# Hybrid encoder layer on one core: the second row tile's LayerNorm moved ahead, v's partial products regrouped, PSUM places swapped

## The chip, the cores and the metric

One core of one Trainium2 chip runs the whole kernel. The metric is the time of one execution in device microseconds, as the median of several runs. An execution's own time is a little more than the span of its instructions, since it includes what lies around them.

## The reference

The input `x` has 1024 positions (a 16 x 64 grid) of 1024 channels, in float32. One LayerNorm (`emb_ln_g`, `emb_ln_b`) gives `h`. One layer follows: `proj = h @ w_in`, split by columns into q, k, v, z_attn, u, z_lru (512 each) and two merge gates (1024 each). Neighbourhood attention with a bias table works on q, k and v; a bidirectional gated linear recurrence works on u. Both results are gated, projected, merged with sigmoid gates and sent through `w_out`, and a second LayerNorm ends the layer:

```python
h = layer_norm(x, emb_ln_g, emb_ln_b)
proj = h @ w_in
q, k, v, z_a, u, z_b, g_a, g_b = jnp.split(proj, offs, axis=-1)
...
return layer_norm(ALPHA * x + out, ln_g, ln_b)
```

The change concerns the first of these steps alone: `h`, its transposed copy, and the first tiles of v and q.

## The kernel before, in words

**Tiles and stages.** The 1024 positions are eight row tiles of 128, numbered 0 to 7. Tile `i` is loaded (`load_x`), normalised on VectorE, stored for later (`keep`, to `h_d`), and turned by TensorE (`turn`) so that channels lie on partitions; a tile has two halves `kk` = 0, 1 of four 128-channel chunks each. Later stages, after about 62 us: the rest of v, q and k-like products, 16 pairs of wide projections in a seven-product scheme (`product`, from 105 us on), the recurrence beside them, then attention, the merges and the output projection.

**High and low parts.** Full precision is made from rounded operands: each float32 operand is split into a rounded high part (ScalarE copies) and a low part, the rest (VectorE or GpSimd subtracts). A product is high x high + low x high + high x low. For v of tile `i`, `v_part(i, kind, ks)` (line 322) issues one 128x512 matmul for each chunk in `ks`: kind `h` is high of h by high of the weight, `a` is low of h by high of the weight, `w` is high of h by low of the weight. Each v tile takes 24 such matmuls into one PSUM bank. They need `turn_hi` (line 278, ScalarE) or `turn_lo` (line 281, VectorE) of the tile's half, and `wv_hi` (line 194, ScalarE) or `wv_lo` (line 197, GpSimd) of the weight chunk. The eight weight chunks come in four transfers of two chunks.

**The first LayerNorm.** Scale and bias are spread into four PSUM banks `gps` (two halves of each). Tiles 0, 1 and 3 read them there: `ln_v(i, c)` (line 240) does one half on VectorE, with the statistics from `ln_stats` (line 216) and the square root from `ln_root` (line 226, ScalarE); `ln_sums` is both. The other tiles are scaled on ScalarE (`ln_scale`, line 248) and finished on GpSimd (`ln_g`, line 255), which reads copies of scale and bias in SBUF; `gb_copy(z, c)` (line 213, ScalarE) makes these, `z` = 0 for the scale and 1 for the bias. Where ScalarE and VectorE read the same PSUM bank, the later reader in program order waits for the earlier one.

**q.** `qk_load(m)` loads a 512 KB weight block into a single buffer, `qk_prep(m)` (line 177) splits it: `qk_hi` casts on ScalarE (line 171) and `qk_lo` subtracts on GpSimd. `qk_load(1)` can start when `qk_lo(0)` has read the buffer, and `qk_prep(1)` comes in ScalarE's order ahead of the high parts of tiles 2 and 3. `q_part(m, n)` multiplies half `n` of the positions; `q_hi` (ScalarE, line 355) and `q_lo` (VectorE, line 360) empty the bank, and the store goes out on SP.

**What sets the order.** Each engine works through its own list in the order in which the code calls the helpers (the order is written out by hand, from line 395 on), and so does the queue SP for the transfers. `warm_up(n)` (line 200) issues `n` matmuls on zeros, which keep TensorE busy while it waits. SP's list is: x0, the weight chunks, x1, more chunks, x2, q's block 0, x3, x4, the small parameters, store of h 0, x5, store of h 1, q's block 1, x6, stores of h 2 and h 3, and so on. x has five buffers, so x5 needs the buffer of x0, and its load waits until the store of h 0 has landed.

**PSUM places.** There are eight banks. While this first part runs, banks 0 to 3 are given out by a list written by hand (`places`, line 86): each call of `bank` takes the next number. Banks 4 to 7 hold `gps` and, after `psg.release()`, the turned tiles 2 to 7. The bank tiles are asked for in this order: clock, tp0_0, and then v0, tp0_1 and so on, as the code first uses them; from v4 on the order is v4, v5, v6, v7, q0_1, q1_1, q2_0, q2_1, q3_0, q3_1 (`q3_1` is `q_part(3, 1)`, the last of them). Then these pools are released, `psd` takes banks 0 and 1 and a pool of six (`ps6`, line 617) takes banks 2 to 7. Its first tile is the first product's accumulator `a11`, in bank 2. A tile in a reused bank waits for the readers of the tile that was there last.

Of the kernel before, what the change touches and what calls it, by code (L numbers as in the profile page):

```python
# [31 lines left out]
WARM = 18, 4, 6  # L32
# [35 lines left out]
def encoder_kernel(ctx, tc, x, gb1, gb, w_qk, w_v, w_s, w_ba, w_bb, w_gate, smalls, bias, w_out, out):  # L68
# [14 lines left out]
    hb12 = pool("hb12", "right")  # L83

    turns = []
    places = itertools.chain((0, 1, 2, 3, 0, 1, 2, 0, 2, 3, 1), itertools.cycle((2, 3, 0, 1)))

    def bank(name):
        if turns:
            return banks[0].tile([P, HALF], F32, tag=next(turns[0]), bufs=2, name=name)  # L90
        if banks[0] is ps0:
            return ps0.tile([P, HALF], F32, tag=f"b{next(places)}", bufs=1, name=name)
        return banks[0].tile([P, HALF], F32, tag="bank", name=name)
# [33 lines left out]
    def lo_of(eng, lo, full, hi):  # L127
        eng.tensor_tensor(lo, full, hi.bitcast(F32), ALU.subtract)  # L128
# [40 lines left out]
    def qk_hi(m):  # L169
        qk_w[m] = pair(wpl, [P, NK, P], f"wqk{m}", tag="w", bufs=2)  # L170
        A.copy(qk_w[m][0][:], qk_s[m][:])

    def qk_lo(m):
        hi, lo = qk_w[m]
        lo_of(G, lo[:], qk_s.pop(m)[:], hi[:])

    def qk_prep(m):
        qk_hi(m)
        qk_lo(m)
# [3 lines left out]
    def load_x(i):  # L183
        xs[i] = ln.tile([P, D], F32, tag="x", bufs=5, name=f"x{i}")
        if i == 0:
            for sl in halves:
                SP.dma_start(xs[i][:, sl], x[i][:, sl])
        else:
            SP.dma_start(xs[i][:], x[i])
# [4 lines left out]
    def wv_hi(k):  # L194
        A.copy(wv[0][k][:], wvs[k // 4][:, k % 4, :])

    def wv_lo(k):
        lo_of(G, wv[1][k][:], wvs[k // 4][:, k % 4, :], wv[0][k][:])

    def warm_up(n):  # L200
        for _ in range(n):
            PE.matmul(clock[:, :P], zero[:], zero[:], start=True, stop=True)
# [10 lines left out]
    def gb_copy(z, c):  # L213
        A.copy(gb_t[z][c][:], gps[z][c][:])

    def ln_stats(i):
        st, mv, e = (ln.tile([P, n], F32, tag=f"ln{n}{c}", bufs=2, name=f"ln{i}{c}")
                     for n, c in ((12, "t"), (2, "m"), (4, "e")))
        sts[i] = st, mv, e[:, 3:4], e[:, 0:3]
        sd, ve = sts[i][2:]  # L220
        for c in range(2):
            V.bn_stats(st[:, 6 * c:6 * c + 6], xs[i][:, halves[c]])
        V.bn_aggr(mv[:], st[:].rearrange("p (c s) -> p c s", c=2))
        V.tensor_scalar(ve[:, 0:1], mv[:, 1:2], EPS, -0.5, ALU.add, ALU.mult)

    def ln_root(i):
        st, mv, sd, ve = sts[i]
        A.activation(sd, mv[:, 1:2], AF.Sqrt, bias=eps_t[:])

    def ln_sums(i):  # L230
        ln_stats(i)
        ln_root(i)

    def ln_rstd(i):
        st, mv, sd, ve = sts[i]
        V.reciprocal(sd, sd)
        V.tensor_scalar(ve[:, 1:2], sd, sd, ve[:, 0:1], ALU.mult, ALU.mult)
        V.tensor_scalar(sd, ve[:, 1:2], 1.5, sd, ALU.add, ALU.mult)

    def ln_v(i, c):  # L240

        z, (st, mv, sd, ve), sl = xs[i], sts[i], halves[c]
        V.scalar_tensor_tensor(z[:, sl], z[:, sl], mv[:, 0:1], gps[0][c][:], ALU.subtract, ALU.mult)
        if c == 0:
            ln_rstd(i)
        V.scalar_tensor_tensor(z[:, sl], z[:, sl], sd, gps[1][c][:], ALU.mult, ALU.add)

    def ln_scale(i):

        z, (st, mv, sd, ve) = xs[i], sts[i]  # L250
        ln_rstd(i)
        V.tensor_scalar(ve[:, 2:3], mv[:, 0:1], -1.0, sd, ALU.mult, ALU.mult)
        A.activation(z[:], z[:], AF.Identity, bias=ve[:, 2:3], scale=sd)

    def ln_g(i):
        z = xs[i]
        for c in range(2):
            for w, op in enumerate((ALU.mult, ALU.add)):
                G.tensor_tensor(z[:, halves[c]], z[:, halves[c]], gb_t[w][c][:], op)

    def keep(i):
        SP.dma_start(h_d[i], xs[i][:])
# [3 lines left out]
    def turn(i, kk):  # L266
        tp = tps[i, kk] = bank(f"tp{i}_{kk}")
        for k4 in range(4):
            k = 4 * kk + k4
            PE.transpose(tp[:, k4 * P:(k4 + 1) * P], xs[i][:, k * P:(k + 1) * P], ident[:])  # L270

    def ti(i):
        return slice((i % 4) * P, (i % 4 + 1) * P)

    def tp4(i, kk):
        return tps[i, kk][:].rearrange("p (k t) -> p k t", k=4)

    def turn_hi(i, kk):
        A.copy(blocks[kk][i // 4][0][:, :, ti(i)], tp4(i, kk))  # L279

    def turn_lo(i, kk):
        hi, lo = blocks[kk][i // 4]
        lo_of(V, lo[:, :, ti(i)], tp4(i, kk), hi[:, :, ti(i)])
# [38 lines left out]
    def v_part(i, kind, ks):  # L322

        if i not in vos:
            vos[i], vn[i] = bank(f"v{i}"), 0
        for k in ks:
            a = blocks[k // 4][i // 4][kind == "a"][:, k % 4, ti(i)]
            PE.matmul(vos[i][:], a, wv[kind == "w"][k][:], start=vn[i] == 0, stop=vn[i] == 23)  # L328
            vn[i] += 1
# [3 lines left out]
    def v_hi(i):  # L333
        vs = outs["v", i] = ln.tile([P, H, 2, DH], F32R, tag="vs", bufs=2, name=f"vs{i}")
        A.copy(vs[:, :, 0, :], vos[i][:].rearrange("p (h d) -> p h d", d=DH))
# [11 lines left out]
    def q_part(m, n, cols=slice(0, HALF)):  # L347
        if (m, n) not in qos:
            qos[m, n] = bank(f"q{m}_{n}")
        run(mm3(qos[m, n][:, cols], [([t[:, 4 * kk + k, :] for t in qk_w[m]], [t[:, k, cols] for t in blocks[kk][n]])  # L350
                                     for kk in range(2) for k in range(4)]))
# [41 lines left out]
    K0, K1, KS, BOTH = range(4), range(4, 8), range(8), range(2)  # L393
# [28 lines left out]
    ln_v(0, 1)  # L422
    keep(0)
    load_x(5)
    turn(0, 1)
    warm_up(WARM[2])
    wv_hi(2)
    wv_hi(3)
    turn_hi(0, 1)
    turn_lo(0, 0)  # L430
    gb_copy(0, 0)
    wv_hi(4)
    wv_hi(5)
    ln_sums(1)
    turn_lo(0, 1)
    wv_hi(6)
    wv_hi(7)
    gb_copy(1, 0)
    for k in KS:
        wv_lo(k)  # L440
    qk_prep(0)
    for k in K0:
        v_part(0, "h", (k,))
        v_part(0, "a", (k,))
    v_part(0, "w", (0, 1))
    v_part(0, "h", (4, 5))
    v_part(0, "w", (2, 3))
    v_part(0, "h", (6, 7))
    v_part(0, "a", K1)
    ln_v(1, 0)  # L450
    ln_v(1, 1)
    keep(1)
    qk_load(1)
    load_x(6)
    turn(1, 0)
    turn_hi(1, 0)
    v_part(0, "w", (4, 5))
    v_part(1, "h", K0)
    turn(1, 1)
    for z in BOTH:  # L460
        gb_copy(z, 1)
    turn_hi(1, 1)
    v_part(0, "w", (6, 7))
    ln_stats(2)
    turn_lo(1, 0)
    ln_root(2)
    v_hi(0)
    ln_scale(2)
    turn_lo(1, 1)
    ln_g(2)  # L470
    v_part(1, "w", K0)
    v_part(1, "h", K1)
    v_part(1, "a", KS)
    v_part(1, "w", K1)
    ln_sums(3)
    q_part(0, 0, slice(0, 256))
    ln_v(3, 0)
# [525 lines left out]
    for slot in range(7 * N_PAIR + 4):  # L1003
        p, k = divmod(slot, 7)
# [183 lines left out]
    for unit in range(-NT, H * NT + PV_LAG):  # L1188
        h, c = divmod(unit, NT)
# [162 lines left out]
    for i in range(NT):  # L1352
        last = i == NT - 1
        load_z(i + 3)
        z = zs.pop(i)
# [115 lines left out]
```

## Time and profile before

| what | value |
|---|---|
| median of 3 runs | 678.17 us (678.04 to 678.44) |
| the profiled execution | 678.46 us |
| its span, first to last instruction | 676.7 us |
| TensorE matmul busy | 665.2 us (98%) |
| TensorE weight loads busy | 555.7 us (82%) |
| VectorE, ScalarE, GpSimd busy | 492.7, 364.5, 355.8 us |
| moved by DMA | 113.39 MB, mean 168 GB/s |
| mean granted TensorE clock | 0.997 |

PE is TensorE's matmuls, PEld its weight loads, DVE is VectorE, ACT ScalarE, POOL GpSimd, and SPq the queue that issues most transfers. In a row of the timeline the columns are the start in us, the duration, the engine, the line, the operation with output and input, and how many instructions are merged; in brackets stands the idle time before it and what ended it. A row of the stages (`A:B`) gives the length, and then the busy time of PE, PEld, DVE, ACT and POOL. In the chain of work that ended last, each row has a start, a duration and what was worked on.

### The profile page before, as it was taken

What the parts mean: (1) busy time and instruction counts of PE and PEld (TensorE: products, weight loads), DVE (VectorE), ACT (ScalarE), POOL (GpSimd) and SP (SyncE); (2) the same over time, 40 slices, a digit from 0 to 9 for tenths busy, and PEclk for the clock granted to TensorE, in tenths of its full rate; (3) what the DMA queues carried; (4) which work ended last, traced back from release to release, by engine and by line L of the source; (5) the groups of instructions that cost most, each with busy time, mean ns of one, the idle gap of its engine ahead of it and who ended that gap; (6) DMA issues with size and microseconds to landing.
All of it is one profiled execution on the core that took longest, in us unless ns stands there. A gap on an engine that the chain in (4) does not pass through costs nothing.

```text
span 676.7 us, 9344 instructions
## 1 busy us (share of the span) xinstructions
PE 665.2 (98%) x3201; PEld 555.7 (82%) x3201; DVE 492.7 (73%) x821; ACT 364.5 (54%) x612; POOL 355.8 (53%) x258
## 2 busy tenths in 40 slices
PE   8999999999999999999999999999999999999995
PEld 6888888888888887888788888888888878888884
DVE  6978747886998699879967785477787787443434
ACT  6554433256786676669576634477777554210110
POOL 6798632434677576567647444116155456334442
PEclk9999999999999999999999999999999999999998
DMA  8654353233434133431553456998793467412211
GB/s 326 244 179 170 122 206 126 77 110 123 125 128 144 40 103 115 170 126 48 195 178 122 173 191 254 316 366 296 255 323 132 162 220 281 178 62 94 93 63 62
DMA packets 48702, 113.39 MB, mean 168 GB/s; under 512 B 5056, under 2 KB 9744, under 8 KB 47120
## 3 DMA queue, kind: packets, MB, share of 16 engines
q1 hardware_dynamic: 48624, 112.81, 47.2%
q8 instruction: 25, 0.41, 0.3%
q14 instruction: 21, 0.17, 0.1%
q10 hardware_dynamic: 32, 0.01, 0.0%
HBM read 77.11 MB, written 35.68 MB: 167 GB/s over the span
## 4 chain that ended last, share of the span: by engine, by line
PE 89%; DVE 6%; DMA 2%; issue 1%; SPq 1%; ACT 0%; POOL 0%; DVEq 0%; POOLq 0%
PE a L134 30%; PE o L134 13%; PE mb L134 12%; PE s L134 11%; PE q L134 6%; PE v L328 6%; PE acc L1107 3%; PE s L1061 3%; PE pt L1083 3%; PE g L759 2%; DMA wqk_s<-in_w_qk_dram 2%; DVE ws_l L128 1%; PE tp L270 1%; DMA rsb<-rs_d 1%; DVE uc L717 1%
## 5 line engine op out<-in xcount | busy, mean ns | idle before, releaser
L134 PE MATMUL o<-wo_h,ml 128*128 128x512 f32 (+1 forms) x136 | 51.2, 377 | 0.0
L134 PE MATMUL o<-wo_l,mh 128*128 128x512 f32 (+1 forms) x136 | 51.2, 376 | 0.0
L134 PE MATMUL o<-wo_h,mh 128*128 128x512 f32 (+1 forms) x136 | 51.2, 376 | 0.0
L134 PE MATMUL a<-ht_h,ws_h 128*128 128x512 f32 x128 | 50.0, 390 | 0.0
L134 PE MATMUL a<-ht_l,ws_h 128*128 128x512 f32 x128 | 49.8, 389 | 0.0
L134 PE MATMUL a<-ht_h,ws_l 128*128 128x512 f32 x128 | 49.8, 389 | 0.0
L134 PE MATMUL a<-b_h,wa_h 128*128 128x512 f32 x128 | 49.8, 389 | 0.0
L134 PE MATMUL a<-b_h,wa_l 128*128 128x512 f32 x128 | 49.8, 389 | 0.0
L134 PE MATMUL a<-b_l,wa_h 128*128 128x512 f32 x128 | 49.8, 389 | 0.0
L1071 DVE CUSTOM_DVE_ANT_0 sc<-s,bias 128x384 f32<-128x384 f32 (+1 forms) x64 | 33.4, 522 | 21.6 <-PE s L1061 14.2
L1361 DVE SCALAR_TENSOR_TENSOR z<-z,o 128x512 f32<-128x512 f32 (+1 forms) x17 | 11.2, 656 | 51.0 <-PE o L134 51.0
L1091 ACT CAST pt_h<-pt 128x384 fp32r<-128x384 f32 x64 | 29.0, 453 | 25.3 <-PE pt L1083 17.3
L1371 POOL TENSOR_TENSOR z<-z,gb 128x1024 f32<-128x1024 f32 x7 | 16.8, 2400 | 48.5 <-ACT z L1370 48.5
L1076 ACT ACTIVATE p<-sc,summ 128x384 f32<-128x384 f32 (+1 forms) x64 | 37.8, 591 | 5.5 <-DVE summ L1071 5.3
L1340 ACT ACTIVATE sd<-mv,eps_z 128x1 f32<-128x1 f32 x8 | 2.4, 294 | 67.1 <-DVE mv L1366 67.1
L128 DVE TENSOR_TENSOR pt_l<-pt,pt_h 128x384 fp32r<-128x384 f32 x64 | 33.2, 519 | 2.1 <-ACT pt_h L1091 1.6
L328 PE MATMUL v<-wv,b_h 128*128 128x512 f32 x128 | 32.9, 398 | 0.6 <-ACT b_h L279 0.5
L867 POOL CAST wb_h<-wb 128x512 fp32r<-128x512 f32 x9 | 7.0, 779 | 47.4 <-DMA wb<-in_w_bb_dram 47.4
L1061 PE MATMUL s<-ks,qs 128*128 128x384 f32 (+1 forms) x128 | 31.4, 327 | 0.0
L1083 PEld LDWEIGHTS pt<-ident,p 128*128 128x128 f32 x176 | 23.1, 140 | 8.5
L1083 PE MATMUL pt<-ident,p 128*128 128x128 f32 x176 | 29.6, 272 | 0.0
L128 POOL TENSOR_TENSOR wb_l<-wb,wb_h 128x512 fp32r<-128x512 f32 x16 | 22.0, 1375 | 14.3 <-ACT wb_h L865 13.6
(438 smaller groups left out, 2204.2 us busy)
## 6 DMA issues: line engine op xcount, KB each, us to landing
ks<-k_d SPq DMA_DIRECT2D x8, 1024.0 KB, 7.5
h_d<-x SPq DMA_DIRECT2D x8, 512.0 KB, 5.0
v_d<-vs SPq DMA_DIRECT2D x8, 512.0 KB, 3.7
q_d<-q SPq DMA_DIRECT2D x8, 512.0 KB, 3.1
ga_d<-ga SPq DMA_DIRECT2D x16, 256.0 KB, 2.2
gb_d<-gb SPq DMA_DIRECT2D x16, 256.0 KB, 2.6
k_d<-k SPq DMA_DIRECT2D x8, 512.0 KB, 3.4
qs<-q_d SPq DMA_DIRECT2D x8, 512.0 KB, 5.5
```

The source lines that it names most:

```text
L128: eng.tensor_tensor(lo, full, hi.bitcast(F32), ALU.subtract)
L134: PE.matmul(o, a, b, start=first and i == 0, stop=last and i == len(prods) - 1, skip_group_check=not (first and last))
L328: PE.matmul(vos[i][:], a, wv[kind == "w"][k][:], start=vn[i] == 0, stop=vn[i] == 23)
L759: PE.matmul(o[:, n, :], w[:, 2 * d + b, :], us[b][:, n * HALF:(n + 1) * HALF], start=z == 0, stop=z == 1)
L1061: PE.matmul(o[:, :P * len(near(t))], q[:, t * P:(t + 1) * P], k[:, z, keys], start=z == 0, stop=z == 1)
L1071: V.tensor_tensor_reduce(s[:, :w], o[:, :w], heads[h][2][:, b0:b0 + w], -1.0, 3.0e38, ALU.add, ALU.min, accum_out=sums[h][0][:, t:t + 1])
L1076: A.activation(probs[h % 2][t][:], scs.pop((h, t))[:, :w], AF.Exp, bias=sums[h][0][:, t:t + 1], scale=-1.0, accum_out=sums[h][1][:, t:t + 1])
L1083: PE.transpose(tp[:, n * P:(n + 1) * P], probs[h % 2][t][:, z * P:(z + 1) * P], ident[:])
L1091: A.copy(pt[0][:, span(b)], tps[h, b][:, :P * len(near(b))])
L1107: PE.matmul(acc[g][:, d:d + w], vvs[h // 2][:, b, h % 2, :], pt[:, a:a + w], start=b in (1, 6) and z == 0, stop=z == 1 and b == (4, 7)[g])
L1361: V.scalar_tensor_tensor(z[:, cols], z[:, cols], ALPHA * TWICE, o, ALU.mult, ALU.add)
L1371: G.tensor_tensor(z[:], z[:], gb2[:, 0, :], ALU.mult)
```

## The change

The calls of the first two tiles are put in another order; no computation is added or taken away but one group of warm-up matmuls.

- Tile 1's statistics and square root come ahead of the second half of tile 0's low part, and `turn_lo(0, 1)` goes between the two halves of tile 1's LayerNorm.
- The four copies of scale and bias are made after tile 1's high parts.
- v's matmuls of tiles 0 and 1 are regrouped: two of tile 0 go ahead of `turn(0, 1)`, in the place of six warm-up matmuls behind it, the rest follow the order in which casts and low parts of the weight chunks come. `v_hi(0)` comes later.
- `qk_prep(0)`, the split of q's first block, goes behind `turn_hi(1, 0)`.
- `places` changes, since v0 is now asked for ahead of tp0_1: 2 and 3 change roles in the list, in its repeating tail too.

```diff
-    places = itertools.chain((0, 1, 2, 3, 0, 1, 2, 0, 2, 3, 1), itertools.cycle((2, 3, 0, 1)))
+    places = itertools.chain((0, 1, 2, 3, 0, 1, 3, 0, 3, 2, 1), itertools.cycle((3, 2, 0, 1)))
...
     load_x(5)
+    v_part(0, "h", (0, 1))
     turn(0, 1)
-    warm_up(WARM[2])
     wv_hi(2)
     wv_hi(3)
     turn_hi(0, 1)
     turn_lo(0, 0)
-    gb_copy(0, 0)
+    ln_stats(1)
     wv_hi(4)
+    ln_root(1)
     wv_hi(5)
-    ln_sums(1)
-    turn_lo(0, 1)
     wv_hi(6)
     wv_hi(7)
-    gb_copy(1, 0)
     for k in KS:
         wv_lo(k)
-    qk_prep(0)
-    for k in K0:
-        v_part(0, "h", (k,))
-        v_part(0, "a", (k,))
-    v_part(0, "w", (0, 1))
-    v_part(0, "h", (4, 5))
-    v_part(0, "w", (2, 3))
-    v_part(0, "h", (6, 7))
-    v_part(0, "a", K1)
+    v_part(0, "h", (2, 3))
+    v_part(0, "a", K0)
+    v_part(0, "w", (0, 1, 2))
+    v_part(0, "h", (4,))
+    v_part(0, "w", (3,))
+    v_part(0, "h", (5,))
+    v_part(0, "w", (4,))
+    v_part(0, "h", (6,))
     ln_v(1, 0)
+    turn_lo(0, 1)
     ln_v(1, 1)
     keep(1)
     qk_load(1)
     load_x(6)
     turn(1, 0)
     turn_hi(1, 0)
-    v_part(0, "w", (4, 5))
+    qk_prep(0)
+    turn_lo(1, 0)
+    v_part(0, "h", (7,))
+    v_part(0, "a", K1)
+    v_part(0, "w", (5,))
     v_part(1, "h", K0)
     turn(1, 1)
-    for z in BOTH:
-        gb_copy(z, 1)
     turn_hi(1, 1)
-    v_part(0, "w", (6, 7))
     ln_stats(2)
-    turn_lo(1, 0)
+    gb_copy(0, 0)
     ln_root(2)
-    v_hi(0)
+    gb_copy(1, 0)
+    turn_lo(1, 1)
     ln_scale(2)
-    turn_lo(1, 1)
+    gb_copy(0, 1)
+    gb_copy(1, 1)
     ln_g(2)
     v_part(1, "w", K0)
+    v_part(1, "a", K0)
+    v_part(0, "w", (6, 7))
     v_part(1, "h", K1)
-    v_part(1, "a", KS)
     v_part(1, "w", K1)
+    v_part(1, "a", K1)
+    v_hi(0)
     ln_sums(3)
```

## The prediction

> **What bounds the kernel now.** I read the page first, then the stages, then the chain of work that ended last over the first 70 us.
>
> ```profile
> span 676.7 us, 9344 instructions
> ...
> PE 665.2 (98%) x3201; PEld 555.7 (82%) x3201; DVE 492.7 (73%) x821; ACT 364.5 (54%) x612; POOL 355.8 (53%) x258
> ...
> PE 89%; DVE 6%; DMA 2%; issue 1%; SPq 1%; ACT 0%; POOL 0%; DVEq 0%; POOLq 0%
> ```
>
> ```profile
> 110.00:285.00 175.00, 175.00 (x770) 143.98 (x769) 150.61 (x182) 112.33 (x140) 100.89 (x74) 1.00 0.34 115
> ```
>
> ```profile
> 16.95 1.19 PE v L328 x4
> ...
> 23.61 2.88 PE q L134 x24
> 26.48 1.75 PE tp L270 x16
> 28.23 9.16 PE v L328 x40
> ```
>
> PE, TensorE's matmuls, is busy 98% of the span, carries 89% of the chain and fills the long stage of products whole (175.00 of 175.00 us), so a microsecond that PE gains or loses early should pass to the end. The chain leaves the transfers for good at 16.95 us: from there PE follows PE. From its rows come my unit costs: a v matmul takes 9.16 / 40 = 0.229 us, the half of q 2.88 us, four transposes 1.75 / 4 = 0.44 us. PE's only real idle time lies ahead of 16.95 us, and it is there that the change works.
>
> **Step 1: the first 23 us, about 1.1 us won.**
>
> ```profile
> 9.19 0.66 PE L270 MATMUL tp<-ident,x 128*128 128x128 f32 x4 [0.52 <-DVE x L246]
> ...
> 10.01 0.58 ACT L279 CAST b_h<-tp 128x512 fp32r<-128x512 f32 x1
> ...
> 11.54 1.14 ACT L195 CAST wv<-wvsl 128x512 fp32r<-128x512 f32 x2 [0.47 <-DMA wvsl<-in_w_v_dram]
> ...
> 11.90 0.68 DVE L128 TENSOR_TENSOR b_l<-tp,b_h 128x512 fp32r<-128x512 f32 x1
> 12.24 5.02 POOL L128 TENSOR_TENSOR wv<-wvsl,wv 128x512 fp32r<-128x512 f32 x4
> 12.49 0.74 DVE L243 SCALAR_TENSOR_TENSOR x<-x,ln1m,gps 128x512 f32<-128x512 f32 x1
> ...
> 14.47 0.75 DVE L246 SCALAR_TENSOR_TENSOR x<-x,ln1e,gps 128x512 f32<-128x512 f32 x1 [0.61 <-ACT gb L214]
> ...
> 15.32 0.63 PE L270 MATMUL tp<-ident,x 128*128 128x128 f32 x4
> ...
> 17.22 2.39 POOL L128 TENSOR_TENSOR wqk_l<-wqk_s,wqk_h 128x1024 fp32r<-128x1024 f32 x1
> ...
> 21.76 5.29 POOL L259 TENSOR_TENSOR x<-x,gb 128x512 f32<-128x512 f32 x4 [2.15 <-ACT x L253]
> ...
> 23.45 0.28 PE L134 MATMUL q<-b_h,wqk_h 128*128 128x256 f32 x1
> ```
>
> Tile 1's LayerNorm (L243, then L246) releases `turn(1, 0)` at 15.32. Two things go from in front of it. `turn_lo(0, 1)` (the 11.90 row) moves behind, so L243 starts at 11.90 instead of 12.49. And L246 no longer idles 0.61 us for a scale-and-bias copy: without that wait it stood 14.47 - 0.61 - 12.49 = 1.37 us behind L243, so it now starts at 13.27 and ends at 14.02. With the 0.06 us that PE took after a VectorE result (8.38 + 0.75 to 9.19, rows here and in step 3), `turn(1, 0)` starts at about 14.1, 1.2 us earlier.
>
> The Trainium skill, "PSUM — Partial Sum Buffer", section "PSUM bank collisions raise a hardware error", says that two engines may not even both read one bank at once and that a kernel has to guard by bank; this trace agrees, since the 0.61 us is VectorE held back from a bank that ScalarE only reads.
>
> Until then PE now issues 16 matmuls of v0. The first two cost `turn(0, 1)` about 0.4 us, but its ScalarE copy stands behind two casts until 10.01 anyway. h4 and h5 wait for their casts (from 11.54, with the root now between them) and w4 for POOL's first low part (12.24 + 5.02 / 4 = 13.50); h6 ends near 13.96. Left are 32 matmuls and two groups of transposes: 32 x 0.229 + 2 x 0.44 = 8.21 us, so q starts near 14.1 + 8.2 = 22.3 instead of 23.45. On the way I find each input in time: `turn_hi(1, 0)` by 15.5, `turn_lo(0, 1)` by 14.7, POOL's last part by 17.26, `turn_hi(1, 1)` by 18.2. The six warm-up matmuls that go stood in time when PE now does real work: nothing. The later copies cost POOL's `ln_g(2)` nothing: VectorE and ScalarE are early by then, and I work it out at 21.2 instead of 21.76.
>
> **Step 2: at 28.95 us the gain meets a transfer, and nothing of it is left.**
>
> ```profile
> SPq L189 <- DMA h_d<-x: 8.6, 1, 8.6
> ```
>
> ```profile
> 19.31 0.33 SPq L189 DMA_DIRECT2D x<-in_x_dram  x1
> ...
> 20.22 0.37 SPq L167 DMA_DIRECT2D wqk_s<-in_w_qk_dram  x1
> ```
>
> ```profile
> 26.21 1.06 ACT L171 CAST wqk_h<-wqk_s 128x1024 fp32r<-128x1024 f32 x1 [1.98 <-DMA wqk_s<-in_w_qk_dram]
> 27.17 1.06 ACT L279 CAST b_h<-tp 128x512 fp32r<-128x512 f32 x2
> 28.12 0.30 ACT L228 ACTIVATE ln4e<-ln4m,eps_t 128x1 f32<-128x1 f32 x1
> 28.32 1.07 ACT L279 CAST b_h<-tp 128x512 fp32r<-128x512 f32 x2
> ```
>
> ```profile
> 28.95 1.21 PEld L328 LDWEIGHTS v<-wv,b_h 128*128 128x128 f32 x6 [0.21 <-ACT b_h L279]
> ```
>
> Tile 2's matmuls need its high parts. ScalarE makes them right behind the cast of q's block 1, which waits for that block's transfer until 26.21; from there ScalarE runs back to back, and the first copy from 28.32 frees the fifth matmul of v2 at 28.95. Even before, its weight load waits 0.21 us for it. ScalarE's order here is the same in both kernels. The transfer is the third that SP issues from 19.31 on; SP stood there 8.6 us for the store of h 0. That store hangs on tile 0 alone, SP's list does not change, and POOL's `qk_lo(0)`, which frees the block's buffer, still follows POOL's last weight part at 17.26 and ends near 17.22 + 2.39 = 19.61, ahead of 20.22. So the landing stays, PE arrives 1.1 us early at the pin and waits: q ends at 25.2, the transposes near 27.4, the first part of v2 waits until 27.7, its second half until 28.95. Gain after this point: 0. If the pin gave way whole it would be 1.1 us.
>
> **Step 3: a new wait at 105 us, 1.68 us lost.**
>
> ```profile
> 8.38 0.75 DVE L246 SCALAR_TENSOR_TENSOR x<-x,ln0e,gps 128x512 f32<-128x512 f32 x1
> ```
>
> ```profile
> 105.18 0.39 PE L134 MATMUL q<-b_l,wqk_h 128*128 128x512 f32 x1
> 105.41 0.39 PE L134 MATMUL a<-b_h,wa_h 128*128 128x512 f32 x1
> ...
> 105.60 0.60 ACT L355 ACTIVATE q<-q 128x512 fp32r<-128x512 f32 x1 [3.82 <-PE q L134]
> ...
> 106.23 0.69 DVE L360 SCALAR_TENSOR_TENSOR q<-q,q 128x512 fp32r<-128x512 f32 x1 [3.55 <-ACT q L355]
> ```
>
> ```profile
> 324.47 0.50 PE L134 MATMUL a<-ht_h,wa_h 128*128 128x512 f32 x1 [0.38 <-DVE w L792]
> 324.81 0.40 PE L134 MATMUL a<-ht_h,wa_l 128*128 128x512 f32 x1
> ```
>
> The list of PSUM places changes in its repeating tail too. Counted from v4, the ten tiles up to q3_1 got 2, 3, 0, 1, 2, 3, 0, 1, 2, 3 and now get 3, 2, 0, 1, 3, 2, 0, 1, 3, 2. So the last q tile, q3_1, moves from bank 3 to bank 2. The pool behind it is not swapped: its first tile, the first product's accumulator, takes bank 2 in both kernels. Before, bank 2 last held q3_0, long emptied, and PE went from q to the product without a break (105.18, 105.41), while ScalarE and VectorE were still reading q3_1 until 106.23 + 0.69 = 106.92. Now the product's first matmul has to wait for that VectorE read; in the built program its wait does name `q_lo(3, 1)`. PE starts at 106.92 + 0.06 = 106.98, 1.57 us late, and the first matmul after a stop takes 0.34 us to the next (324.47, 324.81) instead of 0.23, 0.11 more: **1.68 us**.
>
> Both readers were idle for over 3 us before, so nothing of theirs can come sooner. Behind the waiting matmul stands all of PE. The casts, table load and small operations behind the two reads run on in the wait, but what needs PE's results is late with it. Does a later stage give it back? The one stretch where VectorE leads:
>
> ```profile
> 292.34 0.70 DVE L667 TENSOR_TENSOR a<-u,a 128x512 f32<-128x512 f32 x1 [2.90 <-PE a L134]
> ```
>
> VectorE has just stood 2.90 us for PE there, so it starts as late as PE; I count no absorption. Bounds: 0, if the wait is somehow covered, and 1.7.
>
> The stop could also cost clock. The Trainium skill, "TensorE: Matmul & The Clock Gate", section "HAM oscillation — how this bites in real kernels", warns of PE gaps over some 3.4 us, after which the clock is halved; at 1.6 us it would not bite, and no stop in this trace is long enough to show it (1.00 granted in the stage above).
>
> **Sum.** Against the profiled execution's 678.46 us (span 676.7 and 1.76 around it): step 1 -1.1, taken back in step 2 +1.1, step 3 +1.68, all else 0: 680.14. The median is 0.29 below the profiled execution, so 678.17 + 1.68 = **679.85 us**, slower by 0.25%. About 0.2% (1.36 us) is what a measurement of this kernel can tell from no change.
>
> **The rivals.**
>
> *The pin gives way (not slower by over 0.2%).* If q's block 1 lands, and is cast, 1.1 us sooner, step 1 survives and only 1.68 - 1.1 = 0.58 us is lost: 678.75. It decides at a cast start of about 25.1 instead of 26.21; with over 0.32 us kept, the result is already within 0.2%. For it: the landing hangs on a chain of a store and three transfers, and any change of their overlap moves it. Against it: all of them follow a store that the change does not touch.
>
> *The bank wait is not felt.* If the first product's bank were free, or covered, the time would be that of before, 678.2, or 677.1 with the pin gone too. Against it: the count of places and the two rows at 105.60 and 106.23.
>
> *More is lost.* The stop shifts PE against VectorE and GpSimd through the products, where VectorE has little room (41.34 of 45.00 us busy in the stage below), or costs clock. From the row at 324.47 one such extra stop is 0.4 to 0.8 us; one or two of them give 680.3 to 681.5.
>
> ```profile
> 285.00:330.00 45.00, 44.62 (x196) 36.40 (x196) 41.34 (x37) 31.47 (x40) 30.73 (x19) 1.00 0.30 105
> ```
>
> **How the numbers follow.** Forecast (pin holds, bank wait whole, 679.5 to 680.2): 0.70. Pin gives way in part or whole (678.7 to 679.5): 0.16. Bank wait not felt (677.1 to 678.4): 0.06. More lost (680.3 to 681.5): 0.08. The forecast and the pin's case make 0.86, and the range that holds them with little to spare is 678.7 to 680.3. Over 0.2% slower is above 679.53: the forecast and the case above it, less some of the forecast's lower edge, 0.76. Faster by over 0.2% is below 676.81, under the best case here: 0.01. The rest, 0.23, is within 0.2%.
>
> **What would show it.** Step 1: `turn(1, 0)` near 14.1 and q's first matmul near 22.3. Step 2: ScalarE's cast of q's block 1 still at 26.2 and a PE wait on `b_h` ending at 28.95. Step 3: a PE stop of some 1.2 us in the busy rows at 105.5 to 107.0, ended by L360, and all stages behind it 1.6 to 1.7 us later. I am wrong if the first product's matmul starts within 0.3 us of q's last, if the cast starts before 25.5, or if PE's idle time between 110 and 540 us changes by more than 0.5 us.

## The result, and the profile after

The changed kernel takes 680.53 us (median of 7 runs, 679.18 to 681.27) beside 678.39 us for the kernel before (7 runs, 677.86 to 678.49): ratio 1.0031, 95% interval [1.0019, 1.0042], that is 2.1 us (1.3 to 2.8) slower. The sign and the main cause were foretold, 1.68 us of it; the rest is what the experiments are about. The profiled execution took 680.12 us, 1.66 more than the profiled one of before.

The page of the changed kernel, the same three rows as shown of before:

```profile
span 678.3 us, 9334 instructions
...
PE 665.6 (98%) x3195; PEld 556.6 (82%) x3195; DVE 491.7 (72%) x821; ACT 364.5 (54%) x612; POOL 354.4 (52%) x258
...
PE 89%; DVE 7%; DMA 1%; issue 1%; POOL 1%; ACT 1%; DVEq 0%; POOLq 0%
```

The busy times are the same to a microsecond; what is added is waiting. The stages say where (length, then busy time of PE, PEld, DVE, ACT, POOL):

```profile
105.00:110.00 5.00, 3.59 (x16) 2.63 (x15) 3.12 (x10) 2.60 (x4) 1.29 (x1) 1.00 0.34 106
110.00:285.00 175.00, 175.00 (x771) 144.31 (x771) 148.80 (x181) 111.62 (x140) 99.12 (x73) 1.00 0.33 115
285.00:330.00 45.00, 44.66 (x196) 36.38 (x196) 40.64 (x38) 32.49 (x42) 29.79 (x21) 1.00 0.28 93
```

PE stands 1.41 us between 105 and 110, and the long stage behind it is as full as before, at a granted clock of 1.00. The timeline there:

```profile
105.34 0.39 PE L134 MATMUL q<-b_l,wqk_h 128*128 128x512 f32 x1
...
105.77 0.60 ACT L355 ACTIVATE q<-q 128x512 fp32r<-128x512 f32 x1 [3.81 <-PE q L134]
...
106.40 0.69 DVE L360 SCALAR_TENSOR_TENSOR q<-q,q 128x512 fp32r<-128x512 f32 x1 [3.55 <-ACT q L355]
...
107.14 0.50 PE L134 MATMUL a<-b_h,wa_h 128*128 128x512 f32 x1 [1.41 <-DVE q L360]
...
107.48 0.40 PE L134 MATMUL a<-b_h,wa_l 128*128 128x512 f32 x1
```

From q's last matmul to the first product's first are 1.80 us, where they were 0.23 (105.18 to 105.41): 1.57 more. The matmul starts 0.05 us behind the end of VectorE's read of the same bank (106.40 + 0.69), and the next follows after 0.34. Step 3 of the prediction had these numbers, with 0.06 us where 0.05 was measured.

The first 30 us went otherwise than foretold. The timeline of GpSimd, VectorE, TensorE and ScalarE:

```profile
13.09 5.05 POOL L128 TENSOR_TENSOR wv<-wvsl,wv 128x512 fp32r<-128x512 f32 x4
...
13.65 0.75 DVE L246 SCALAR_TENSOR_TENSOR x<-x,ln1e,gps 128x512 f32<-128x512 f32 x1
...
14.43 0.73 PE L328 MATMUL v<-wv,b_h 128*128 128x512 f32 x2 [0.46 <-DVE x L246]
...
15.01 0.60 PE L270 MATMUL tp<-ident,x 128*128 128x128 f32 x4
...
22.02 5.28 POOL L259 TENSOR_TENSOR x<-x,gb 128x512 f32<-128x512 f32 x4 [1.53 <-ACT x L253]
...
23.23 0.28 PE L134 MATMUL q<-b_h,wqk_h 128*128 128x256 f32 x1
...
25.67 1.06 ACT L171 CAST wqk_h<-wqk_s 128x1024 fp32r<-128x1024 f32 x1 [1.61 <-DMA wqk_s<-in_w_qk_dram]
...
28.30 1.05 ACT L279 CAST b_h<-tp 128x512 fp32r<-128x512 f32 x2
```

And the chain there (start, duration, what; in the chain a matmul starts some 0.2 us later than in the timeline, and v2's starts are the chain's throughout):

```profile
27.36 1.09 PE tp L270 x8
28.45 9.11 PE v L328 x40
```

The transposes of tile 1's first half (the x4 row) start at 15.01, not at 14.1; q comes at 23.23, not at 22.3; v2 starts at 28.45, 0.22 us later than before, behind transposes that waited for GpSimd's x of tile 2 (22.02 + 5.28 = 27.30). At 14.43 two releases fall together: VectorE's x is done at 14.40, GpSimd's fifth low part of the weights, which the matmul of that row reads, at about 13.09 + 5.05 / 4 = 14.35. The row names the later one, though the matmul does not read x, so this execution alone does not tell which of the two held it.

### The profile page after: what moved, and what is told of

Read it like the earlier page. It is cut to its first block, busy times and chain, and to the rows that moved or that the text cites. A ratio compares the mean times of both kernels' runs of the same rounds, so it can differ in the third digit from the quotient of the medians.

```text
span 678.3 us, 9334 instructions
## 1 busy us (share of the span) xinstructions
PE 665.6 (98%) x3195; PEld 556.6 (82%) x3195; DVE 491.7 (72%) x821; ACT 364.5 (54%) x612; POOL 354.4 (52%) x258
## 4 chain that ended last, share of the span: by engine, by line
PE 89%; DVE 7%; DMA 1%; issue 1%; POOL 1%; ACT 1%; DVEq 0%; POOLq 0%
PE a L134 29%; PE o L134 13%; PE mb L134 12%; PE s L134 11%; PE q L134 6%; PE v L328 5%; PE acc L1111 3%; PE s L1065 3%; PE pt L1087 3%; PE g L763 2%; DVE ws_l L128 1%; PE tp L270 1%; DMA rsb<-rs_d 1%; POOL x L259 1%; DVE uc L721 1%
## 5 line engine op out<-in xcount | busy, mean ns | idle before, releaser
L134 PEld LDWEIGHTS a<-b_h,wa_h 128*128 128x128 f32 x128 | 24.0, 188 | 6.8 <-DVE q L360 1.8
```

The costliest lines, as they stand in the source:

```text
L134: PE.matmul(o, a, b, start=first and i == 0, stop=last and i == len(prods) - 1, skip_group_check=not (first and last))
```

## The experiments

In the edits, "old places" is `places` changed so that q3_1 gets bank 3 again. All ratios are to the kernel before, run on the same chip beside it; a ratio need not be the exact quotient of the two medians given with it. Theories A to C are stated in the expectations.

### The two parts of the change apart

**e1, the changed kernel with the old places at q3_1.**

```diff
-    places = itertools.chain((0, 1, 2, 3, 0, 1, 3, 0, 3, 2, 1), itertools.cycle((3, 2, 0, 1)))
+    places = itertools.chain((0, 1, 2, 3, 0, 1, 3, 0, 3, 2, 1), (3, 2, 0, 1) * 2, (2, 3))
```

> The changed kernel, but with the last two q tiles' PSUM banks exchanged, so that q3_1 lies in bank 3 again and the first product's bank holds q3_0. Theory A (two causes: the bank wait costs 1.6 to 1.85 us, and the rest of the loss of 2.1 us comes from the first 30 us, where the new order lies open to how late TensorE's clock comes up): the stop at 105 us is gone, the median is 678.4 to 679.1 us, and single runs still spread over more than 1 us. Theory B (everything is lost by the stop at 105 us and what follows from it): 678.2 to 678.5 us, that of before, with the narrow spread of before (0.6 us). Theory C (the early order itself costs, the bank wait is small): over 679.5 us.

Measured: 679.04 us (before 678.23), ratio 1.0011 [1.0001, 1.0021]. The early order alone costs about 0.8 us (0.1 to 1.4 by the interval); the prediction had it at nothing. The median lies in theory A's box, at its upper end.

**e2, the kernel before with the new places at q3_1.**

```diff
-    places = itertools.chain((0, 1, 2, 3, 0, 1, 2, 0, 2, 3, 1), itertools.cycle((2, 3, 0, 1)))
+    places = itertools.chain((0, 1, 2, 3, 0, 1, 2, 0, 2, 3, 1), (2, 3, 0, 1) * 2, (3, 2))
```

> The kernel before, with one thing changed: q3_0 and q3_1 exchange their PSUM banks, so that the first product's accumulator takes the bank that q3_1 has just left. Theory A: 1.6 to 1.85 us slower than before, 680.0 to 680.25 us, with the narrow spread of before. Theory B: 2.1 us slower, about 680.5 us, with the wide spread of the changed kernel (over 1.5 us). Theory C: under 679.3 us.

Measured: 679.88 us, ratio 1.0025 [1.0015, 1.0035]: 1.65 us between the medians, where step 3 had 1.68. That is 0.12 us below theory A's box, and far from B's and C's. The wait stands in its row (engine, line, waited for: us, times, longest):

```profile
PE a L134 <- DVE q L360: 1.4, 1, 1.4
```

**e3 and e4: TensorE started later.** Twelve more warm-up matmuls ahead of tile 0's transposes, in the kernel before (e3) and in e1's kernel (e4):

```diff
-    warm_up(WARM[2])
+    warm_up(WARM[2] + 12)
     ln_sums(0)
```

> The kernel before with twelve more warm-up matmuls ahead of the first tile's transposes, which hold these back by 0.6 to 1.3 us as a late clock does. Theory A (in the old order the first 30 us are timed by transfers, so a late start of TensorE is hidden): 678.4 to 678.9 us, under 0.5 us slower than before. Theory B (start-up plays no part in either kernel): 678.4 us here and no cost in the next run either.

> The same twelve warm-up matmuls in the changed kernel with the bank wait undone. Theory A (the new order is timed by the chain from tile 0 over tile 1's LayerNorm to tile 2 on GpSimd, so a late start passes on): 0.5 to 1.2 us slower than the kernel with the bank wait undone alone. Theory B: within 0.2 us of it.

Measured: e3 678.36 us, ratio 1.0001 [0.9991, 1.0011]; e4 678.51 us, ratio 1.0006 [0.9995, 1.0017]. In their profiles tile 0's transposes start at 9.19 us in e3 (7.68 before) and at 8.33 in e4 (7.89 in e1), so e4's start was held back by less than was meant. A later start costs the kernel before nothing that shows, and in the new order the time is, if anything, below e1's. So nothing shows that the 0.8 us comes from how TensorE starts, as theory A had it, and by e1 and e2 together it does not come from the stop at 105 us alone. A new theory was needed.

### Theory D: the early order is tied to GpSimd

In the new order one matmul, w4 of v0, stands ahead of the transposes of tile 1's first half, and it reads GpSimd's fifth low part. GpSimd makes its eight parts from the landing of the first weight chunk on, and that landing moves from execution to execution. The parts follow each other, but for one possible wait in the middle, for ScalarE's next casts: 0.24 us in before, 0.60 in the changed kernel's profile, none in e1. e1's timeline:

```profile
13.30 5.03 POOL L128 TENSOR_TENSOR wv<-wvsl,wv 128x512 fp32r<-128x512 f32 x4
...
14.64 0.74 PE L328 MATMUL v<-wv,b_h 128*128 128x512 f32 x2 [0.50 <-POOL wv L128]
...
15.21 0.60 PE L270 MATMUL tp<-ident,x 128*128 128x128 f32 x4
```

and its chain from there to v2, which starts 15.37 us behind the start of the first of these rows:

```profile
13.30 1.30 POOL wv L128
14.64 0.74 PE v L328 x2
15.81 2.32 PE v L328 x10
18.60 0.60 ACT b_h L279
19.22 0.69 DVE b_l L128
20.91 1.25 ACT x L253
22.23 1.30 POOL x L259
...
27.58 1.09 PE tp L270 x8
28.67 9.12 PE v L328 x40
```

Here the wait has GpSimd's name, and the chain shows the path: from the fifth low part over w4 and the matmuls behind it to tile 1's second copy, VectorE's low part of it, the scaling of tile 2, GpSimd's finish of tile 2, its transposes, and v2. Four edits on e1's kernel test this, against the rival that the loss arises later (R2).

**e5, w4 and h6 behind the transposes.**

```diff
-    v_part(0, "w", (4,))
-    v_part(0, "h", (6,))
     ln_v(1, 0)
...
     turn(1, 0)
+    v_part(0, "w", (4,))
+    v_part(0, "h", (6,))
     turn_hi(1, 0)
```

> The changed kernel with the old list of places, and on TensorE the fifth low-weight matmul of v0 (w4) and the h6 behind it moved from ahead of the transposes of tile 1's first half to right behind them. Theory D (the early order gains nothing, because w4 stands ahead of these transposes and needs GpSimd's fifth low part, which comes only some 5 us plus 1.3 us after GpSimd's first): the transposes now wait for the LayerNorm alone and start at 14.0 to 14.3 us, where the kernel with only the places undone had 15.21; q's first matmul comes near 22.7 instead of 23.44. The second tile's x from GpSimd is not touched, so v2 still starts near 28.4, and the median stays 0.4 to 0.9 us above the kernel before. Rival R1 (LayerNorm or the first half of TensorE's list sets it, not w4): the transposes stay at 14.9 to 15.3.

Measured: 679.39 us (before 678.90), ratio 1.0010 [1.0001, 1.0019]; 0.49 us above the kernel before and in theory D's box. The transposes start at 14.67, later than expected: the landing was late in this execution (fifth low part at 13.87), w3 ahead of them waits for the fourth part until 13.97, and VectorE's x is done at 13.82 + 0.75 = 14.57. By e1's distance (15.21 - 13.30 = 1.91) they would have started at 15.78, and v2 comes 14.92 us behind the fifth part instead of 15.37. The tie moved by one part; it was not cut.

**e6, tile 2's scaling ahead, as it stood before.**

```diff
-    gb_copy(0, 0)
     ln_root(2)
+    gb_copy(0, 0)
+    ln_scale(2)
     gb_copy(1, 0)
     turn_lo(1, 1)
-    ln_scale(2)
```

> The changed kernel with the old list of places, and the square root and the scaling of tile 2 put back ahead of the low part of tile 1's second half on VectorE and ahead of the copies of scale and bias on ScalarE, as they stood in the kernel before; nothing else. Theory D (tile 2's normalised x comes late from GpSimd because the small operations now stand behind that low part): GpSimd's finish of tile 2 starts near 21.6 us instead of 22.23, v2 starts near 28.1 instead of 28.67, and the median is 0.1 to 0.5 us above the kernel before, where the kernel with only the places undone was 0.8 above. Rival R2 (the 0.8 us arises after 60 us, from transfers that shift): landmarks as said, but the median stays 0.7 to 0.9 us above.

Measured: 679.42 us, ratio 1.0014 [1.0004, 1.0024]; GpSimd's finish of tile 2 starts at 21.30 and v2 at 27.91, earlier than before. The landmarks are theory D's. The median, 0.52 us above the kernel before (0.95 by the ratio), does not decide: D's box ends at 0.5, R2's begins at 0.7.

**e7, both edits.**

> Both edits together: w4 and h6 behind the transposes of tile 1's first half, and tile 2's scaling ahead. Theory D: q's first matmul near 22.7 us, v2's first near 27.6, and then the pin of the prediction's step 2: the second half of v2 waits for ScalarE's last high parts, behind the cast of q's second block at about 26, until about 29. Median between 0.3 us below and 0.4 us above the kernel before. Rival R2: 0.7 to 0.9 us above, whatever the landmarks.

Measured: 679.85 us, ratio 1.0015 [1.0005, 1.0024]; q at 23.39, v2 at 28.31. The landmarks came later than expected, with a late landing (fifth part at 13.70), and the median, 0.95 us above the kernel before, is just above R2's box and far from D's.

**e8, both edits and the pin of step 2 taken away.**

```diff
-    v_hi(0)
     ln_sums(3)
+    v_hi(0)
...
     v_hi(1)
-    qk_prep(1)
...
-    ln_sums(4)
+    ln_stats(4)
...
     turned_in(3, 1)
+    ln_root(4)
+    qk_prep(1)
     ln_scale(4)
```

> As the kernel with both edits, and on ScalarE the cast of q's second block and the square root of tile 4 moved behind the high parts of tiles 2 and 3, the square root of tile 3 ahead of v0's cast. Theory D with the prediction's step 2: no wait is left on v2's second half, v2 runs through from about 27.5 us, and the median is 0.3 to 1.0 us below the kernel before. Rival R2: no gain from it, within 0.3 us of the kernel with both edits. Rival R3 (the later low part of q's second block and the later scaling of tile 4 hold up a later stage): the gain at 28 us is there, but given back by 45 us.

Measured: 680.25 us, ratio 1.0019 [1.0009, 1.0028], a miss: theory D expected a gain. The gain at 28 us is not there either, since v2 starts at 28.24 in the timeline, where 27.5 was expected (fifth part at 13.97). GpSimd's timeline:

```profile
30.46 2.42 POOL L128 TENSOR_TENSOR wqk_l<-wqk_s,wqk_h 128x1024 fp32r<-128x1024 f32 x1 [3.15 <-ACT wqk_h L171]
32.83 22.27 POOL L259 TENSOR_TENSOR x<-x,gb 128x512 f32<-128x512 f32 x16
55.06 5.03 POOL L128 TENSOR_TENSOR ht_l<-t,ht_h 128x512 fp32r<-128x512 f32 x4
```

The low part of q's second block starts 3.11 us later than before (27.35), and from there GpSimd works without a gap until 60 us; the chain runs through it to TensorE, which stands 0.19 us for the last of this work, until 62.38. GpSimd, 53% busy over the span, has little to spare there: in before it idles 1.04 and 0.45 us between 28 and 58. That is R3's path, though later than the 45 us it named. Its price is not shown: the median is 0.4 us above e7's, the intervals overlap, and e8 has the race of the next section as well.

### Theory L: a race at 92 us

e7's chain leaves TensorE a second time, and its waits have one row on q:

```profile
PE q L134 <- DVE q L360: 0.6, 1, 0.6
```

The timeline of before, and then of e7, at VectorE's last sum of the first product's weights and GpSimd's low part:

```profile
92.38 0.68 DVE L380 TENSOR_TENSOR s_0f<-a_0f,s_0f 128x512 f32<-128x512 f32 x1
...
92.40 1.82 POOL L128 TENSOR_TENSOR wa_l<-a_0f,wa_h 128x512 fp32r<-128x512 f32 x1 [1.81 <-ACT wa_h L385]
```

```profile
92.86 1.33 POOL L128 TENSOR_TENSOR wa_l<-a_0f,wa_h 128x512 fp32r<-128x512 f32 x1 [1.70 <-ACT wa_h L385]
...
92.95 1.78 DVE L380 TENSOR_TENSOR s_0f<-a_0f,s_0f 128x512 f32<-128x512 f32 x1
```

The two rows start within 0.1 us of each other, and it is a race which of the two engines gets in first. In before VectorE is first: its sum takes 0.68 us, GpSimd's part 1.82. In e7 GpSimd is first: 1.33, and the sum takes 1.78. VectorE is then 1.1 us late with q's bank, as e7's chain shows:

```profile
92.95 1.78 DVE s_0f L380
94.74 0.61 DVE q L360
95.40 11.18 PE q L134 x48
106.58 8.16 PE a L134 x36
```

TensorE, whose q began at 73.06 and takes 32.64 us without a wait (before), would have ended it at 105.70; it starts the product at 106.58. The profiles of e1, e2, e7 and e8 show the sum at 1.78. Those of before, after, e5 and e6 show it at 0.68 or 0.69 with the two rows 0.02 us apart or less, and those of e3 and e4 at 0.68, where GpSimd's part came 0.75 and 1.37 us later. So this race goes either way in the old order (e2) as in the new. Four kernels without it: VectorE makes this one part (f1 in the kernel before, f2 in e1's, f3 in e6's, f4 in e7's).

```diff
-            lo_of(G if o in LO_POOL else V, lo[:], s_a[p, o][:], hi[:])
+            lo_of(G if o in LO_POOL and (p or o != "a11") else V, lo[:], s_a[p, o][:], hi[:])
```

> The kernel before, with one low part of the first product's weights (a11 of pair 0, read by GpSimd at about 92.5 us) made by VectorE instead of GpSimd; nothing else. Theory L (at 92.4 to 93.0 us VectorE's last sum of the first weights and GpSimd's low part are ready within 0.1 us of each other; both read two operands from SBUF, one holds the other up, and where GpSimd comes first the sum takes 1.78 us instead of 0.68, and TensorE then waits 0.4 to 1.0 us for q's bank): the last sum takes 0.68 us, no TensorE wait on q between 90 and 106 us, the median is up to 0.3 us below the kernel before and the upper half of the times comes closer. Rival S (the scatter comes from transfers): no change in median or spread.

> The same edit in the changed kernel with the old list of places. Theory L with theory D: only the later start of v2 is left (0.2 to 0.5 us), so the median is 0.1 to 0.5 us above the kernel before, where the same order with the race was 0.8 above. Rival S: 0.7 to 0.9 above, as with the race.

> The same edit in the kernel with tile 2's scaling ahead. Theory L with theory D: v2 starts near 27.9 us, 0.3 earlier than in the kernel before, and nothing takes it back: median 0.1 to 0.6 us below the kernel before. Rival S: 0.4 to 1.0 above.

> The same edit in the kernel with both early edits (w4 behind the transposes and tile 2's scaling ahead). Theory L with theory D: v2 near 27.6 to 28.3 by the landing of the first weights, no wait at 90 to 106 us, median between 0.6 us below and 0.2 us above the kernel before. Rival S: 0.5 to 1.0 above, as with the race.

| kernel | median us (before 678.91) | ratio | the same with the race |
|---|---|---|---|
| f1, before | 678.72 | 1.0000 [0.9992, 1.0009] | 1 |
| f2, new order | 679.05 | 1.0003 [0.9994, 1.0012] | e1 1.0011 [1.0001, 1.0021] |
| f3, scaling ahead | 679.16 | 1.0005 [0.9996, 1.0014] | e6 1.0014 [1.0004, 1.0024] |
| f4, both | 679.28 | 1.0000 [0.9990, 1.0010] | e7 1.0015 [1.0005, 1.0024] |

The sum takes 0.68 or 0.69 us in all four, and none of the four has a TensorE wait there. All three ratios of the new order fall, by 0.5 to 1.0 us, but the intervals overlap, so a gain is likely and not shown. Of the medians f2's (0.14 us above the kernel before) lies in theory L's box; f3's and f4's (0.25 and 0.37 above) lie above it and below rival S's. In f1 the ratio is 1 and the times spread as before (677.92 to 679.93), so in the old order nothing of a gain shows.

The profiles give the race a price. From the end of v2's row of 40 matmuls to the start of the first product, both in the chain, 68.15 to 68.18 us pass in the eleven profiles that have neither the race nor the bank's wait; in e1 it is 68.55 and in e7 69.04. So the race cost 0.4 us in e1 and 0.9 in e7, and without it this stretch is the same in both orders.

### The tie itself

Set side by side, the profiles give theory D a sharper form. Start of GpSimd's fifth low part, start of v2, difference, and end of v2's row of 40 matmuls:

| order | execution | fifth part | v2 | difference | end of the 40 |
|---|---|---|---|---|---|
| new | e4 | 13.03 | 28.40 | 15.37 | 37.52 |
| new | after | 13.09 | 28.45 | 15.36 | 37.56 |
| new | e1 | 13.30 | 28.67 | 15.37 | 37.79 |
| new | f2 | 13.68 | 29.05 | 15.37 | 38.16 |
| old | before | 12.24 | 28.23 | 15.99 | 37.39 |
| old | e2 | 13.05 | 28.17 | 15.12 | 37.62 |
| old | f1 | 13.27 | 28.11 | 14.84 | 37.23 |
| old | e3 | 13.53 | 28.73 | 15.20 | 38.36 |

In the new order v2 follows GpSimd to 0.01 us. The edits of e5 to e7 move the distance, and it repeats: 14.92 in e5, 15.05 in e6 and in f3, 14.61 in e7 and in f4. In the old order GpSimd can come 1 us later and v2 does not move (f1's timeline and chain, then e2's chain):

```profile
13.27 5.04 POOL L128 TENSOR_TENSOR wv<-wvsl,wv 128x512 fp32r<-128x512 f32 x4
```

```profile
15.25 1.05 ACT wqk_h L171
...
28.11 9.12 PE v L328 x40
```

```profile
15.31 1.05 ACT wqk_h L171
...
28.17 9.45 PE v L328 x40
```

What v2 hangs on there is another transfer: the cast of q's first block waits for that block to land, and tile 1's copies stand behind it on ScalarE. The cast starts at 15.37 us in before, 15.31 in e2 and 15.25 in f1, and v2 12.86 us later in all three. The change moved this cast behind tile 1's first copy, and so gave up a landing that moved by 0.12 us for one that moves by more. In e3, where TensorE's transposes of tile 0 began 1.5 us late, v2 waited instead for the cast of q's second block, at 27.15.

A later start of v2 is not all loss. e2's 40 matmuls take 9.45 us instead of 9.12, since they wait inside for step 2's pin, and end later than those of e4 and of the changed kernel at nearly the same fifth part. Over the executions of the table the new order ends them at 37.52 to 38.16 and the old one at 37.23 to 37.62, or 38.36 with e3.

Two times that move together can have a common cause, so three more kernels were run.

**g2, GpSimd makes the first low part twice (f2's kernel).**

```diff
+    wv_lo(0)
     for k in KS:
         wv_lo(k)
```

> The changed kernel with the old list of places and without the race at 92 us, and GpSimd makes v's first low weight part twice, so that its whole list stands about 1.25 us later; the landing of the weights and everything ahead of it are untouched. Theory D in its last form (w4 ties TensorE to GpSimd: in the four executions of this order seen so far, v2 starts 15.36 to 15.37 us behind the start of GpSimd's fifth low part): v2 starts 15.3 to 15.5 us behind that part again, now at 29.5 to 30.3 us, and the median is 1.0 to 1.4 us above the same kernel with one such part, some 680.2. Rival S2 (both are late by a common cause, such as the traffic of transfers in the first 10 us, and neither hangs on the other): v2 stays at 28.4 to 29.1, the median near 679.05.

Measured: the fifth part starts at 14.66, v2 at 30.01, 15.35 behind (timeline and chain):

```profile
14.66 5.03 POOL L128 TENSOR_TENSOR wv<-wvsl,wv 128x512 fp32r<-128x512 f32 x4
```

```profile
30.01 9.12 PE v L328 x40
```

Only GpSimd was touched and v2 came with it: the tie is a cause, not a coincidence, and S2 falls. The median is 681.50 us (before 678.87; 6 runs, 679.48 to 682.37), ratio 1.0041 [1.0027, 1.0054]: 2.4 us above f2, where 1.0 to 1.4 was expected. The profiled executions differ by 1.1 (spans 678.6 and 677.5); why the median moves by more is not settled.

**g3, the low-weight matmuls from w2 on put later (f3's kernel).**

```diff
-    v_part(0, "w", (0, 1, 2))
-    v_part(0, "h", (4,))
-    v_part(0, "w", (3,))
-    v_part(0, "h", (5,))
-    v_part(0, "w", (4,))
-    v_part(0, "h", (6,))
+    v_part(0, "w", (0, 1))
+    v_part(0, "h", (4, 5, 6))
...
-    v_part(0, "w", (5,))
+    v_part(0, "w", (2, 3))
...
-    v_part(1, "w", K0)
     v_part(1, "a", K0)
-    v_part(0, "w", (6, 7))
+    v_part(1, "w", K0)
+    v_part(0, "w", (4, 5))
     v_part(1, "h", K1)
-    v_part(1, "w", K1)
+    v_part(0, "w", (6, 7))
     v_part(1, "a", K1)
+    v_part(1, "w", K1)
```

> The kernel with tile 2's scaling ahead and without the race, and on TensorE the low-weight matmuls of v0 from the third on are put where GpSimd can hardly be late: w2 and w3 behind the transposes of tile 1's first half, w4 to w7 behind those of its second half. Theory D: the transposes of tile 1's first half start at 14.0 to 14.3 us whatever the first weights do, q's first matmul near 22.8, v2 at 27.5 to 28.2, where GpSimd's finish of tile 2 or the cast of q's second block holds it; v2 minus the start of the fifth low part is no constant any more. Median between 0.5 us below the kernel before and 0.1 above. Rival S2: 0.2 to 0.5 above, as the same kernel with the old places of these matmuls.

Measured: 678.76 us, ratio 0.9997 [0.9988, 1.0006], in theory D's box, the lowest of the new orders and not told apart from the kernel before. The execution had one of the latest landings (fifth part at 14.10). The transposes started at 14.88, not held by GpSimd: the matmul right ahead of them had waited for a cast until 14.22, and VectorE's x was done at 14.03 + 0.75 = 14.78. The expected 14.0 to 14.3 is a miss, and so is v2's 27.5 to 28.2: it started at 28.65, and its chain shows by what:

```profile
19.14 2.39 POOL wqk_l L128
...
21.55 5.49 DMA wqk_s<-in_w_qk_dram
...
27.07 1.05 ACT wqk_h L171
...
28.65 9.61 PE v L328 x40
```

That is step 2's pin. Its transfer waits for GpSimd's low part of q's first block (19.14 + 2.39 = 21.53, issued at 21.55), so a late GpSimd moves the pin as well, and with it the old order: SP's issue follows that low part by 0.03 us in e2 and 0.02 in f1 too.

**g4, the whole change without the race.**

> The changed kernel whole, only without the race at 92 us. Theory L with D: the bank's wait (1.65 us) and the tie to GpSimd (0.2 to 0.8) are left: median 1.8 to 2.3 us above the kernel before, and v2 15.3 to 15.4 us behind GpSimd's fifth low part. If the parts don't add up (rival: the bank's wait is shorter or longer when TensorE comes later), the median lies outside of 1.4 to 2.7 above.

Measured: 681.09 us, ratio 1.0030 [1.0019, 1.0041], 2.2 us between the medians (2.0 by the ratio), within the 1.8 to 2.3 that the parts give. In its profile the fifth part starts at 14.17 and v2 at 29.52 (15.35), and from q's end to the first product 1.40 us pass (106.79 to 108.19). Its twelve runs go from 678.60 to 682.06.

## Why the prediction was right or wrong

**Step 3 was right**, mechanism and size: 1.57 us of wait measured where 1.57 was worked out, 0.34 to the next matmul, 1.65 us in the median when the places alone are changed (e2). Hardly anything of it came back behind: the VectorE row at 292.34 came at 293.93 (L667 before, L671 after), 1.59 us later.

**Step 1 is the step that failed**, mainly in one term: "w4 for POOL's first low part (12.24 + 5.02 / 4 = 13.50)". The 12.24 was read from one execution and used as a property of the kernel. It hangs on the landing of a transfer: ScalarE's cast of the first chunk started at 6.22 us in that execution, at 6.78 in the changed kernel's, and at 7.00 to 8.48 in the fifteen others profiled here. GpSimd's wait for the next casts, 0.60 us instead of 0.24, added to it. In the changed kernel the fifth part was done at 14.35, and w4 and h6 put the transposes at 15.01 instead of 14.1. Of these 0.9 us the LayerNorm itself has 0.4, since its x was done at 14.40 against 14.02 (at 13.95 in e1). So q's first matmul came 0.22 us earlier than before (23.23), not 1.1.

A second term of step 1 failed with it: `ln_g(2)` "at 21.2 instead of 21.76" came at 22.02. VectorE's small operations for tile 2 now stand behind `turn_lo(1, 1)`, and I had only looked at the copies on ScalarE. e6 undoes that alone: measured from the fifth part, GpSimd's finish comes 0.49 us earlier (21.30 - 12.86 beside 22.23 - 13.30) and v2 0.32 us (15.05 beside 15.37).

**Step 2 held for another reason than given.** Nothing of a gain passed 28 us, but the pin named there (the cast of q's second block at 26.2, a wait on `b_h` until 28.95) was not what held v2: the cast came at 25.67, v2's 40 matmuls ran without a wait inside (9.11 us), and GpSimd's x of tile 2 was later. Nor did the transfer hang on the store alone: its issue at 20.52 followed GpSimd's low part of q's first block (18.08 + 2.42 = 20.50), which the prediction had at 19.61. So steps 1 and 2 together were not "gain back to 0" but a loss, 0.22 us at v2's start in the profile, 0.17 at the end of its 40 matmuls, and 0.8 in e1's median, the race at 92 us included. By the distance of 15.37 us v2 in the new order starts no later than in the old one (28.17, e2) only where GpSimd's fifth part starts by 12.80. Of the 17 profiled executions only that of before (12.24) lay under it.

**The sum.** Of the 0.68 us by which the median lies above the forecast, 0.22 is the kernel before itself (678.39 beside the forecast's 678.17). 1.65 (e2) and 0.8 (e1) make 2.5 against 2.14 measured, within the intervals. The profiled execution shows 1.57 and 0.17 and is 1.66 above. That it meets the prediction's sum for it (680.14) to 0.02 us is luck: the landing was early and VectorE won the race at 92 us. What of e1's 0.8 is the tie and what the race was not separated, and stays open: f2's interval holds both 0 and 0.8. Behind the first product, too, the rest of the span takes 570.3 to 571.7 us in the 17 profiles, and this scatter, larger than the 0.8, is not explained.

**The rivals.** "More is lost" was the right box at 8%, but it was priced from VectorE's lack of room after 285 us, and that did not happen (PE was busy 44.66 of 45.00 us there, 44.62 before). "The bank wait is not felt" is excluded by e2. "The pin gives way" is excluded by the changed kernel's profile and by e1: the cast did come 0.54 us sooner, and v2 came later all the same. No version that was tried beats the kernel before by what can be measured.

## What to carry to other kernels

Before a time from a trace becomes a term of a sum, ask what it hangs on: here the landing of the first weights moved by 2.3 us, and an order that ties TensorE to it inherits that, while an order that waits for a transfer with a steadier landing inherits less. Take differences between events of one execution (15.37 us, whatever the landing) rather than clock readings, and lay several executions side by side where there are some. And when a list of PSUM places is changed, count it to its end: the price stood 80 us behind the edit, in a pool that the change did not touch.

## What the runs showed of the hardware that was not expected

The first weight chunk, the third transfer of a fixed list on one queue, was ready for its cast between 6.22 and 8.48 us in 17 profiled executions, a spread of 2.3 us. In the new order v2 moves with it. What moves the landing is not shown, nor is it shown that it makes the scatter of the times: the kernel before, whose v2 does not hang on it, also went from 677.49 to 680.92 us in the 35 runs beside e5 to e8. The landing of q's first block, a later transfer of the same queue, let its cast start between 15.25 and 15.37 us in the four profiles of the old order's early part that wait for it.

VectorE and GpSimd block each other when both read two operands from SBUF: the same sum takes 0.68 us when it is first and 1.78 when GpSimd is, the same low part 1.33 and 1.82. The Trainium skill, "SBUF — State Buffer", section "SBUF: two separate sides", says that the pair of ports between them is a lock held for a whole instruction, and that an operation of VectorE with two SBUF inputs competes for it only with a GpSimd operation that reads SBUF; the rows above agree, since 92.86 + 1.33 = 94.19 and the blocked sum ends 0.54 us later, at 94.73, about its own length. Which of the two came first was settled by 0.02 us in before and 0.25 us in e2, and TensorE reached the first product 0.4 us (e1) to 0.9 us (e7) later where it was GpSimd.
